# One transpose task for both token tiles of a normed projection, and tasks due close together issued together

## Chip, cores and metric

The kernel runs on one core of a Trainium2 chip. The metric is the device time of one execution in microseconds; a lower time is better. The time of before is the median of three runs. The profile is of one further execution.

## What is computed

Two layers of a decoder trunk over 256 tokens of width 1024. Each layer is a half-weighted SwiGLU feed-forward (hidden width 2816), a mixing stage with two groups of eight heads of 64 (group A in the code's order of work is the second half of the heads), and a second feed-forward. All of it is in float32. The mixing stages, cut to what matters here:

```python
def mix_stick_moba(xn, w_in, g_q_b, g_k_b, cos, sin):          # layer 0
    q, k, v = ...                                              # xn @ w_in, split in three, by heads
    out_a = stick_breaking_attention(q[:, :H_A], k[:, :H_A], v[:, :H_A])
    q_b = apply_rope(rms_norm(q[:, H_A:], g_q_b), cos, sin)
    k_b = apply_rope(rms_norm(k[:, H_A:], g_k_b), cos, sin)
    out_b = moba_attention(q_b, k_b, v[:, H_A:])
    ...

def mix_forget_dilated(xn, w_in, b_f, g_q_c, ..., cos, sin):   # layer 1
    log_f = log_sigmoid(proj[..., 3 * D_MIX:] + b_f)
    q_c = rms_norm(q[:, :H_C], g_q_c)                          # k_c likewise
    out_c = forgetting_attention(q_c, k_c, v[:, :H_C], log_f)
    q_d = apply_rope(rms_norm(q[:, H_C:], g_q_d), cos, sin)    # k_d likewise
    out_d = dilated_window_attention(q_d, k_d, v[:, H_C:])
    ...
```

A *normed projection* is a q or k that goes through `rms_norm` by head, with or without rope after it. There are six: q and k of the rope heads in both layers, and q and k of the forgetting heads in layer 1. They are called q2, k2 (rope) and q1, k1 (without).

## The kernel before, in words

The 256 tokens are two tiles of 128 (t = 0, 1). Weights stream in on the SP queue in units of 1 MB. Each unit is split into a high and a low part: ScalarE casts the high part (line 248), and VectorE subtracts it to get the low part (line 249). A projection is then three matmuls for each piece of weights, in `mm3` (line 149 is the one place that issues matmuls).

`token_major` projects 512 columns: first all of tile 0 (24 matmuls), then all of tile 1, and calls `done(t, ps)` after each. `project_norm` (line 481) uses it for a normed projection. Its `norm(t, ps)` squares on ScalarE (line 488), reduces on VectorE, takes a power on GpSimd (line 228), scales on VectorE into `qn` (line 493), and with rope forms `qs` on VectorE (lines 500 and 501) with products by GpSimd in between (line 498). The tags `qn`, `qs` and `sq` have two buffers each. Then TensorE transposes the tile, in 8 transposes (line 165, function `transposes`), into `tt`, a pair of PSUM banks of which there is one buffer, and ScalarE casts it into half of `qT` or `kT` (line 506).

The order on TensorE is written by hand; the other engines' order is left to the framework's scheduler. A small planner, `Weave`, keeps a clock `pe.t` that grows with each matmul by an assumed cost (its columns divided by 2400) and by 0.065 for a pair of transposes. Side work is a generator that is spawned as a task with a due time; where it yields x, it is due again x us later. `poll` is called after every three projection matmuls, and runs each task whose due time has passed, the earliest first. `join` runs tasks until given ones are done. `norm` is such a task: it yields 14 us (`LEAD_R`, with rope) or 10 us (`LEAD_N`) between its norm and its transposes, so that the norm is done by then.

A `Group` is the attention of eight heads and also a task, in six steps 6 us apart: scores `a` of a head pair (into two z banks, of which there are two buffers), transposes of the softmax `b` of the pair before, product `c` of the pair before that. The first group, A, waits until all norm tasks of q2 and k2 are done, looking every 0.2 us; the second, B, waits for q1, k1 and until A has issued four steps. In layer 1, `forget` also spawns a task: a chain over `lgy` on VectorE and ScalarE (lines 539 to 544), two small transposes (line 548), a cumulative sum of three small matmuls, and small copies.

In layer 0 the order in mixing is q2, k2, v2, q1, k1, v1, and the output projection of A, then that of B. In layer 1, `forget` stands between v2 and q1.

Of the kernel before, what the change touches and what calls it, by code (L numbers as in the profile page):

```python
# [11 lines left out]
AF = mybir.ActivationFunctionType  # L12
# [4 lines left out]
P = 128  # L17
TAIL = 3
LEAD_R, LEAD_N, LEAD_F, OVER = 14.0, 10.0, 8.0, 4
LEAD_X = (1.5, 1.5)  # L20
LEAD_0 = 3.0
PACE = ((6.0, 6.0), (6.0, 6.0))
HP = P // 2
D = 1024
KT = D // P
DFF = 2816
# [51 lines left out]
class Weave:  # L78
# [17 lines left out]
            self.tasks.remove(task)  # L96

    def poll(self):
        while self.tasks:
            task = min(self.tasks, key=lambda k: k[0])  # L100
            if task[0] > self.t:
                return
            self._run(task)

    def join(self, *tasks):
        while not all(k[2] for k in tasks):
            task = min(self.tasks, key=lambda k: k[0])
            self.t = max(self.t, task[0])
            self._run(task)
# [3 lines left out]
def trunk(ctx, tc, a, out):  # L113
    nc = tc.nc
# [12 lines left out]
    def nm(s):  # L127
        seen[s] = seen.get(s, 0) + 1
        return f"{s}_{seen[s]}"
# [13 lines left out]
    def pair():  # L143

        return psum.tile([P, 2, 512], F32, tag="tt", bufs=1, name=nm("tt"))
# [11 lines left out]
    def transposes(*srcs):  # L157

        tb, n, vs = pair(), 0, []
        for src in srcs:  # L160
            n0 = n
            for j in range(src.shape[-1] // P):
                for b in range(2):
                    r = slice(b * HP, (b + 1) * HP)
                    nc.tensor.transpose(tb[:, b, n * HP:(n + 1) * HP], src[r, j * P:(j + 1) * P], ident[r, r])  # L165
                n += 1
                pe.t += 0.065
            vs.append(tb[:, :, n0 * HP:n * HP].rearrange("p b (c t) -> p c b t", t=HP))
        return vs

    def halves(v):

        return v.rearrange("p c (b t) -> p c b t", t=HP)


    x = [keep.tile([P, D], F32, name=f"x{t}") for t in range(2)]
    ident = const.tile([P, P], F32, name="ident")
# [93 lines left out]
    class Normed:  # L271
# [16 lines left out]
        def transpose(self, t):  # L288
            tk, halfs = slice(t * P, (t + 1) * P), [slice(h * 512, (h + 1) * 512) for h in range(2)]
            for h, v in enumerate(transposes(*[x[t][:, sl] for sl in halfs])):  # L290
                kk = slice(4 * h, 4 * h + 4)
                xg = xpool.tile([P, 4, P], F32, tag="xg", bufs=2, name=nm("xg"))
                nc.vector.tensor_mul(halves(xg), v, self.g[:, kk].unsqueeze(2).unsqueeze(3).to_broadcast([P, 4, 2, HP]))  # L293
                nc.scalar.copy(self.hi[:, kk, tk], xg)  # L294
# [4 lines left out]
        def inverse(self, t):  # L299
            junk = xpool.tile([P, D], BF, tag="junk", name=nm("junk"))  # L300
            ss = small.tile([P, 1], F32, tag="ss", name=nm("ss"))
            nc.scalar.activation(junk, x[t], AF.Square, accum_out=ss)
            self.r[t] = rpow(ss, D, 1)
            if self.rb is None:
# [40 lines left out]
    def row_gemm(lhs, src, row0, tail, n_units, done, tasks=()):  # L345
# [16 lines left out]
        for u in range(n_units):  # L362
            r0 = row0 + 2 * u * P
            units.append(unit(src[r0:r0 + 2 * P, :].rearrange("(k p) n -> p k n", p=P), [2, D]))
            if u == 2:
# [90 lines left out]
    def _mix(mp, layer, xt, gains, done):  # L456
        def new(tag, width=512, bufs=2, dt=F32):
            return mp.tile([P, width], dt, tag=tag, bufs=bufs, name=nm(tag))
# [22 lines left out]
        def project_norm(c0, g, tag):  # L481
            qT = mp.tile([P, 4, SEQ], F32, tag=tag, bufs=2, name=nm(tag))
            tasks = []
            rope = isinstance(g, tuple)

            def norm(t, ps):
                sq = new("sq")
                nc.scalar.activation(sq, ps, AF.Square, scale=xt.r[t])
                ss = small.tile([P, 8], F32, tag="hss", name=nm("hss"))
                nc.vector.tensor_reduce(ss, heads(sq), axis=AX.X, op=ALU.add)  # L490
                r = rpow(ss, HD, 8)
                qn = new("qn")
                nc.vector.scalar_tensor_tensor(heads(qn), heads(ps), xt.r[t],  # L493
                                               r.unsqueeze(2).to_broadcast([P, 8, HD]), op0=ALU.mult, op1=ALU.mult)
                if rope:
                    gc, gs = g
                    o, sw = new("qs"), new("sq")
                    half_swap(lambda u, v: nc.gpsimd.tensor_mul(  # L498
                        heads(sw)[:, :, u], heads(qn)[:, :, v], over_heads(gs[:, t, u])))
                    nc.vector.tensor_mul(heads(o), heads(qn), over_heads(gc[:, t]))  # L500
                    nc.vector.tensor_add(o, o, sw)
                    yield LEAD_R
                else:
                    o = qn
                    yield LEAD_N
                nc.scalar.activation(halves(qT[:, :, t * P:(t + 1) * P]), transposes(o)[0], AF.Copy,
                                     scale=1.0 if rope else g)

            token_major(xt, w, c0, acc, lambda t, ps: tasks.append(pe.spawn(norm(t, ps))))
            return qT, tasks  # L510
# [210 lines left out]
        q2, tq = project_norm(cb, gq, "qT")  # L721
        k2, tk = project_norm(D + cb, gk, "kT")
        tc.keep_in_program_order(nc.scalar.preload_act_table_set("natural_log_exp_and_others"))
# [78 lines left out]
```

## Time and profile before

| | |
|---|---|
| median of three runs | 1029.31 us (1028.9 to 1030.21) |
| the profiled execution | 1029.01 us |
| span of the profile, first to last instruction | 1027.2 us |
| mean granted TensorE clock | 0.993 |
| TensorE busy | 1003.0 us, 5410 matmuls and transposes |
| VectorE busy | 603.3 us |
| ScalarE busy | 497.7 us |
| GpSimd busy | 87.9 us |

The span covers the two layers: mixing lies at about 198 to 324 us in layer 0 and at 698 to 836 us in layer 1, the rest is feed-forward. PE is TensorE, PEld its weight loads, DVE VectorE, ACT ScalarE, POOL GpSimd. A granted clock of 1.00 is TensorE at 2.4 GHz, 0.50 is 1.2 GHz. In the rows further down, a timeline row has the start in us, the time from the first to the last instruction in it, the engine, the line, and what was written from what; "[0.24 <-ACT pT L681]" is idle time ahead of it and what ended that. Matmuls overlap, so the step from one start to the next is what one costs in a row of them.

### The profile page before, as it was taken

Reading aid. Unit: us, or ns where it says so; the run is one execution under the profiler, and the core shown is the slowest. Engines: PE = TensorE matmul, PEld = TensorE weight load, DVE = VectorE, ACT = ScalarE, POOL = GpSimd, SP = SyncE. Lnnn points to the kernel's source line nnn. Section 1 sums busy time; section 2 is a strip of 40 time slices with the busy share of each in tenths; the row PEclk is TensorE's granted clock in tenths of the full one; section 3 lists DMA queues with packets and bytes.
Section 4 is the critical chain, followed back from the end, with each engine's and each line's share of the span. In section 5 each row is a group of like instructions: output and inputs, shape, how many; then the busy total and the mean of one; then the engine's idle time right before and its main releaser. Section 6 shows DMA issues by size and latency. Waiting matters only on the chain.

```text
span 1027.2 us, 13525 instructions
## 1 busy us (share of the span) xinstructions
PE 1003.0 (98%) x5410; PEld 833.3 (81%) x5410; DVE 603.3 (59%) x798; ACT 497.7 (48%) x669; POOL 87.9 (9%) x110
## 2 busy tenths in 40 slices
PE   7999999999999999999999999999999799999998
PEld 5888988779777888988878899887766678889886
DVE  6655554687676554564565546448876855546641
ACT  6554543555665444454454445336645555444530
POOL 0000200051000000000040000006431000000000
PEclk9999999999999999999999999999989999999999
DMA  9744475454233653655464456545523425535631
GB/s 331 266 154 153 159 284 187 158 187 165 83 127 123 211 185 123 215 212 198 142 230 164 150 178 245 185 145 196 175 84 103 144 82 194 205 124 205 216 123 41
DMA packets 81935, 175.95 MB, mean 171 GB/s; under 512 B 4544, under 2 KB 21264, under 8 KB 81872
## 3 DMA queue, kind: packets, MB, share of 16 engines
q1 hardware_dynamic: 80208, 174.86, 50.2%
q8 instruction: 42, 0.69, 0.3%
q0 software_dynamic: 512, 0.17, 0.2%
q10 hardware_dynamic: 1152, 0.06, 0.1%
q14 instruction: 21, 0.17, 0.0%
HBM read 173.99 MB, written 1.05 MB: 170 GB/s over the span
## 4 chain that ended last, share of the span: by engine, by line
PE 88%; DVE 6%; ACT 2%; issue 1%; POOL 1%; DMA 1%; SPq 0%; ACTq 0%; DVEq 0%; POOLq 0%
PE acc L149 54%; PE z L149 25%; PE o L149 6%; DVE lo L249 3%; PE tt L165 3%; ACT hi L248 1%; PE tt L149 1%; POOL rp L228 1%; POOL sq L498 1%; DMA raw<-in_w_in_ab 1%; DVE mx L663 0%; ACT t L669 0%; DMA x<-in_x 0%; DVE qn L493 0%; DVE xg L293 0%
## 5 line engine op out<-in xcount | busy, mean ns | idle before, releaser
L249 DVE TENSOR_TENSOR lo<-raw,hi 128x1024 fp32r<-128x1024 f32 (+2 forms) x348 | 403.4, 1171 | 240.5 <-ACT hi L248 229.8
L248 ACT CAST hi<-raw 128x1024 fp32r<-128x1024 f32 (+2 forms) x348 | 344.6, 1001 | 293.8 <-PE z L149 124.8
L149 PE MATMUL acc<-hi,xt 128*128 128x512 f32 (+1 forms) x1088 | 344.6, 387 | 3.9 <-ACT xt L294 2.1
L149 PEld LDWEIGHTS acc<-hi,xt 128*128 128x128 f32 x1088 | 204.4, 190 | 43.4 <-DVE xt L295 4.4
L149 PE MATMUL z<-hi,xt 128*128 128x512 f32 (+1 forms) x768 | 226.5, 371 | 0.0
L149 PE MATMUL acc<-lo,xt 128*128 128x512 f32 (+1 forms) x544 | 207.1, 381 | 0.0
L149 PEld LDWEIGHTS z<-hi,xt 128*128 128x128 f32 x768 | 142.4, 188 | 20.0
L149 PE MATMUL z<-lo,xt 128*128 128x512 f32 (+1 forms) x384 | 142.3, 371 | 0.0
L149 PEld LDWEIGHTS acc<-lo,xt 128*128 128x128 f32 x544 | 103.5, 190 | 15.6 <-DVE lo L249 0.2
L149 PE MATMUL acc<-hi,hh 128*128 128x512 f32 x264 | 103.6, 392 | 0.0
L149 PE MATMUL acc<-hi,hl 128*128 128x512 f32 x264 | 102.9, 390 | 0.0
L149 PE MATMUL acc<-lo,hh 128*128 128x512 f32 x264 | 102.8, 389 | 0.0
L228 POOL TENSOR_TENSOR rp<-ms,mhalf 128x1 f32<-128x1 f32 (+1 forms) x24 | 31.9, 1328 | 618.8 <-DVE ms L226 618.7
L149 PEld LDWEIGHTS z<-lo,xt 128*128 128x128 f32 x384 | 72.1, 188 | 9.9
L394 DVE TENSOR_TENSOR h<-z,sg 128x512 f32<-128x512 f32 (+1 forms) x48 | 30.9, 643 | 54.5 <-PE z L149 54.5
L149 PEld LDWEIGHTS acc<-hi,hh 128*128 128x128 f32 x264 | 49.5, 188 | 10.4
L149 PEld LDWEIGHTS acc<-hi,hl 128*128 128x128 f32 x264 | 49.5, 188 | 10.4
L149 PEld LDWEIGHTS acc<-lo,hh 128*128 128x128 f32 x264 | 49.5, 188 | 10.0
L390 ACT ACTIVATE sg<-acc,rp 128x512 f32<-128x512 f32 (+1 forms) x48 | 31.4, 654 | 41.3 <-PE acc L149 40.6
L263 ACT CAST hh<-tt 128x512 fp32r<-128x512 f32 (+1 forms) x48 | 26.5, 551 | 46.4 <-PE tt L165 26.7
L264 DVE TENSOR_TENSOR hl<-tt,hh 128x512 fp32r<-128x512 f32 (+1 forms) x48 | 31.0, 646 | 21.7 <-ACT hh L263 21.4
L149 PE MATMUL o<-hi,hh 128*128 128x512 f32 x88 | 34.4, 391 | 0.0
(144 smaller groups left out, 799.1 us busy)
## 6 DMA issues: line engine op xcount, KB each, us to landing
raw<-in_ffn_w_down SPq DMA_DIRECT2D x44, 1024.0 KB, 5.0
raw<-in_ffn_w_up SPq DMA_DIRECT2D x32, 1024.0 KB, 5.1
raw<-in_ffn_w_gate SPq DMA_DIRECT2D x30, 1024.0 KB, 5.1
raw<-in_ffn_w_gate SPq DMA_DIRECT2D x16, 768.0 KB, 4.4
raw<-in_ffn_w_up SPq DMA_DIRECT2D x16, 768.0 KB, 4.4
raw<-in_w_in_ab SPq DMA_DIRECT2D x12, 1024.0 KB, 5.3
raw<-in_w_in_cd SPq DMA_DIRECT2D x12, 1024.0 KB, 5.2
raw<-in_w_out SPq DMA_DIRECT2D x8, 1024.0 KB, 5.0
```

The source lines that it names most:

```text
L149: nc.tensor.matmul(o, lhsT, rhs, start=start, stop=stop, skip_group_check=True)
L165: nc.tensor.transpose(tb[:, b, n * HP:(n + 1) * HP], src[r, j * P:(j + 1) * P], ident[r, r])
L228: nc.gpsimd.tensor_tensor(r, m, mhalf[:, :width], op=ALU.pow)
L248: nc.scalar.copy(hi[:, j:j + m], w[:, i * n + j:i * n + j + m])
L249: nc.vector.tensor_sub(lo[:, j:j + m], w[:, i * n + j:i * n + j + m], hi[:, j:j + m].bitcast(F32))
L263: nc.scalar.copy(halves(hi), v)
L264: nc.vector.tensor_sub(halves(lo), v, halves(hi).bitcast(F32))
L390: nc.scalar.activation(sg[t][:, :n], pg[:, :n], AF.Silu, scale=xt.r[t])
L394: nc.vector.tensor_mul(hs[t][:, :n], pu[:, :n], sg[t][:, :n])
L498: half_swap(lambda u, v: nc.gpsimd.tensor_mul(heads(sw)[:, :, u], heads(qn)[:, :, v], over_heads(gs[:, t, u])))
```

## The change

`norm` of tile 0 now ends after the norm, and that of tile 1 transposes both tiles, in one set of 16, and casts both halves. `poll` also runs, after each task that it runs, all other tasks that are due within the next 0.5 us.

```diff
+SOON = 0.5
...
     def poll(self):
         while self.tasks:
             task = min(self.tasks, key=lambda k: k[0])
             if task[0] > self.t:
                 return
             self._run(task)
+            for k in sorted(self.tasks, key=lambda k: k[0]):
+                if k is not task and k[0] <= self.t + SOON and k in self.tasks:
+                    self._run(k)
...
+            outs = []
+
             def norm(t, ps):
...
                     nc.vector.tensor_add(o, o, sw)
-                    yield LEAD_R
                 else:
                     o = qn
-                    yield LEAD_N
-                nc.scalar.activation(halves(qT[:, :, t * P:(t + 1) * P]), transposes(o)[0], AF.Copy,
-                                     scale=1.0 if rope else g)
+                outs.append(o)
+                if t == 0:
+                    return
+                yield LEAD_R if rope else LEAD_N
+                for i, v in enumerate(transposes(*outs)):
+                    nc.scalar.activation(halves(qT[:, :, i * P:(i + 1) * P]), v, AF.Copy, scale=1.0 if rope else g)
```

## Rows read from the trace of the kernel before

**Rows 1.** The page's busy times, share of the span, instructions.
```profile
PE 1003.0 (98%) x5410; PEld 833.3 (81%) x5410; DVE 603.3 (59%) x798; ACT 497.7 (48%) x669; POOL 87.9 (9%) x110
```

**Rows 2.** Windows: stretch, its length, each engine's busy time, granted clock, DMA share, GB/s.
```profile
192.00:262.00 70.00, 69.30 (x463) 59.01 (x462) 55.89 (x88) 40.01 (x68) 20.40 (x15) 1.00 0.49 166
...
691.00:775.00 84.00, 79.92 (x459) 62.32 (x459) 69.02 (x142) 48.22 (x72) 36.34 (x33) 0.96 0.43 139
...
740.00:742.00 2.00, 0.65 (x7) 0.44 (x6) 1.21 (x2) 1.42 (x4) 0.00 (x0) 1.00 1.01 357
...
762.00:766.00 4.00, 4.00 (x10) 3.13 (x11) 1.20 (x4) 0.69 (x1) 0.00 (x0) 0.50 0.02 4
775.00:785.00 10.00, 8.41 (x47) 5.52 (x45) 6.14 (x12) 4.19 (x6) 2.07 (x1) 0.83 0.60 211
```

**Rows 3.** Waits of PE from 690 to 840: total, times, longest.
```profile
PE z L149 <- ACT kT L506: 2.1, 2, 1.4
```

**Rows 4.** Timeline of PE, layer 0, around a set of 16 and one of 8.
```profile
199.08 0.39 PE L149 MATMUL acc<-lo,xt 128*128 128x512 f32 x1
...
200.00 0.39 PE L149 MATMUL acc<-hi,xt 128*128 128x512 f32 x1
200.31 0.71 PE L165 MATMUL tt<-ident,x 64*128 64x64 f32 x16
...
201.29 0.40 PE L149 MATMUL acc<-lo,xt 128*128 128x512 f32 x1
...
221.17 0.39 PE L149 MATMUL acc<-hi,xt 128*128 128x512 f32 x1
221.49 0.47 PE L165 MATMUL tt<-ident,qs 64*128 64x64 f32 x8
...
222.22 0.39 PE L149 MATMUL acc<-lo,xt 128*128 128x512 f32 x1
```

**Rows 5.** Timeline of ACT and PE, layer 0, the last kT cast and A's first scores.
```profile
240.07 0.60 ACT L506 ACTIVATE kT<-tt 128x512 f32<-128x512 f32 x1 [3.43 <-PE tt L165]
...
241.10 0.92 PE L149 MATMUL z<-kT,qT 64*128 64x256 f32 x8
```

**Rows 6.** Timeline of DVE, ACT and PE, layer 1, ahead of A's first scores.
```profile
738.88 0.41 DVE L539 TENSOR_TENSOR lgy<-acc,rb 8x256 f32<-8x256 f32 x1
...
739.70 0.42 ACT L541 ACTIVATE lge<-lgy 8x256 f32<-8x256 f32 x1 [2.20 <-DVE lgy L540]
...
740.91 0.57 ACT L506 ACTIVATE kT<-tt 128x512 f32<-128x512 f32 x1
...
741.54 0.92 PE L149 MATMUL z<-kT,qT 64*128 64x256 f32 x8 [1.35 <-ACT kT L506]
```

**Rows 7.** Timeline of PE and DVE, layer 0: q2's second set, k2's first `qs`.
```profile
227.55 0.46 PE L165 MATMUL tt<-ident,qs 64*128 64x64 f32 x8
...
228.29 1.23 DVE L500 TENSOR_TENSOR qs<-qn,gc 128x512 f32<-128x512 f32 x1
```

**Rows 8.** Timeline of PE, layer 1: transposes that wait.
```profile
758.21 0.51 PE L165 MATMUL tt<-ident,t 64*128 64x64 f32 x6 [1.27 <-DVE t L673]
...
761.30 0.69 PE L165 MATMUL tt<-ident,qn 64*128 64x64 f32 x8 [0.24 <-ACT pT L681]
761.92 0.79 PE L149 MATMUL acc<-hi,xt 128*128 128x512 f32 x1
...
772.34 0.46 PE L165 MATMUL tt<-ident,qn 64*128 64x64 f32 x8 [0.76 <-ACT pT L681]
...
778.34 0.60 PE L165 MATMUL tt<-ident,t 64*128 64x64 f32 x6 [1.59 <-DVE t L673]
```

**Rows 9.** Timeline of PE and DVE, layer 0: B's first scores, A's last transposes.
```profile
268.99 0.27 PE L149 MATMUL z<-negb,identb 128*128 128x256 bf16 x1 [1.26 <-ACT t L669]
...
270.20 1.01 DVE L673 TENSOR_SCALAR t<-t,l 128x128 f32<-128x128 f32 x4
...
272.09 0.59 PE L165 MATMUL tt<-ident,t 64*128 64x64 f32 x12
```

## The prediction, made before the changed kernel ran

> **What bounds the kernel now.** I read the page's busy times first: TensorE is busy for 98% of the span, so a change of its instruction order is worth what it takes from, or adds to, TensorE's own sequence [rows 1]. Next the windows by stage: the change acts in the two mixing stages alone. In layer 0's, TensorE is busy 69.3 of 70 us; in layer 1's first part only 79.9 of 84 us, and there VectorE is busy 69.0 us [rows 2]. So layer 0 is bound by TensorE, and layer 1 partly by what VectorE and ScalarE hand to it. The waits and timelines say where: for the kT casts (line 506) 2.1 us in two waits [rows 3], of which 1.35 us stand ahead of group A's first scores [rows 6]; for the softmax ahead of A's transposes 1.27 and 1.59 us, and for the `tt` banks 0.24 and 0.76 us ahead of two transposes of qn [rows 8].
>
> **The order that the change makes.** I worked it out from the planner's due times (0.213 us of its clock for a 512-column matmul, a poll after every three). All four feed-forward parts keep their order. In mixing, each of six projections has its two sets of 8 transposes replaced by one set of 16, where about the second stood. The 0.5 us rule moves three things: in layer 0, A's last transposes and third product join group B's first scores, with 0.7 us less of matmuls between A's last scores and them than before; in layer 1, the lgy transposes follow A's first transposes instead of preceding A's second scores, so the cumulative sum stands alone; and A's later steps no longer drag the first set of q1 behind them. The sum is made against the profiled execution, 1029.01 us (span 1027.2), which is 0.3 us under the median of the runs, 1029.31.
>
> *One set of transposes among projection matmuls.* Matmuls follow each other at (200.00 - 199.08)/4 = 0.23 us. A set of 8 stretches the two steps around it to 222.22 - 221.17 = 1.05 us, 0.59 more than 0.46. A set of 16 takes 201.29 - 200.00 = 1.29, 0.83 more [rows 4]. Joining two sets saves 2 x 0.59 - 0.83 = 0.35 us of TensorE. Layer 0 has two joined sets: **-0.7** (ends: -0.7, and 0 if TensorE then waits anyway).
>
> *The second cast, layer 0.* Both halves of kT are now cast after the 16 transposes. Before, A's scores began at 241.10 and the one cast, 0.60 us, started at 240.07, with 0.43 us to spare [rows 5]. One more cast of 0.60 overshoots by 0.17: **+0.2** (ends 0 and +0.6). The casts of qT are read 10 us later and cost nothing; if that cover were gone, 0.6 us each.
>
> *B's first scores with A's last transposes, layer 0.* TensorE waits 1.26 us for the z bank at 268.99, and the transposes at 272.09 follow softmax divisions that end at 270.20 + 1.01 [rows 9]. Issued together, the break into the matmuls goes once less (about half of the 0.59 above, 0.3), but the transposes come up before the divisions are done, so that most of the wait moves there: **-0.4** (ends: -1.7, wait and break both gone, and +0.6, the transposes wait out the divisions).
>
> *Layer 1's rope projections.* TensorE would again save 0.7 us, but A's first scores start when the kT cast ends; that cast stands behind ScalarE's share of lgy, which begins at 739.70, and this behind VectorE's lgy at 738.88 [rows 6]. An earlier TensorE only waits longer: 0. With two casts behind them, +0.57, the duration in that row: **+0.6** (ends: -2.05, 0.7 and the whole 1.35, if both casts run ahead of lgy's share; +1.15 if one more instruction as long as the cast stands between).
>
> *A's steps, layer 1.* Between A's second scores and their transposes there are three matmuls fewer, and these transposes wait already (1.27) [rows 8]: 3 x 0.23 = +0.7. For its last transposes the cover grows by the 8 more of the joined set, 0.25: -0.25. The cumulative sum's own break, from nothing to 0.59: +0.2, as it has 3 small matmuls and no bank to wait for. Together **+0.6** (ends 0 and +1.0).
>
> *q1.* Its first set, from 761.30 to the next matmul at 761.92 [rows 8], goes out of A's step: -0.6. The second, with its 0.76 us wait, costs 0.59 + 0.76 = 1.35 and becomes a set of 16 without that wait, 0.83; but these 0.5 us stand ahead of A's last transposes, which wait for VectorE anyway (1.59). **-0.6** (ends -1.1 and 0).
>
> *k1 and group B.* -0.35 for the join; B's first scores already wait the rest of the 2.1 us, 0.75 [rows 3], for one cast, and a second adds about 0.7, as these casts carry a gain (up from 0.6 in [rows 5], and no more than twice that): **+0.35** (ends -0.35 and +0.85).
>
> *Buffers.* `qs` has two buffers, held until the joined transposes. k2's first write of `qs` came at 228.29, after q2's second set at 227.55 [rows 7], where the joined set will be: 0 (a VectorE wait of 0.3 at most, covered by splits done ahead; without this cover 0.3). The planner adds no DMA and moves none on a queue; the evacuations keep their number.
>
> The sum is -0.7 + 0.2 - 0.4 + 0.6 + 0.6 - 0.6 + 0.35 = 0.05 us, nothing that shows: I take 1029.1 us. The ends add to -5.9 and +4.2.
>
> The Trainium skill, page "Perfetto Trace Analysis", section "Optimizing Scalar/DVE Operations", says that where these engines aren't saturated but cause bubbles elsewhere, breaking instructions up may let work complete sooner; joining is the opposite. The trace bears it out in kind: ScalarE is busy 48%, and its kT casts hold TensorE up. By that rule alone the sum would be the three second casts, +1.5 us; by the rows it is offset.
>
> **Rivals.** *Faster.* The joins count in full and ScalarE takes the two casts ahead of the lgy chain: -0.7 - 0.4 - 2.05 - 1.1 - 0.35 + 0.6 + 0.2 = -3.8. If in addition the last wait of A shrinks, and the clock stays up there, more: that stretch has a granted clock of 0.83, and at the half level (1.2 GHz, [rows 2]) 10 matmuls took 4.0 us, 0.4 each instead of 0.23. Ten at half clock are 1.7 us. Time: 1025.3, or 1023.6. For it: TensorE's 98%. Against it: the scheduler put the cast behind the lgy chain once already.
>
> *Slower.* A's first scores in layer 1 wait for two casts, and the granted clock falls to the half level behind that wait, as it did behind the waits of 1.27 and 0.24 us up to 761.30 and around the 1.59 us wait [rows 2, 8]. The wait there is now 1.35, and the clock is at its full level, 2.4 GHz (1.00 from 740 to 742) [rows 2, 6]. With 1.95 us in its place it could fall: 10 to 16 matmuls at 0.17 more, 1.7 to 2.7 us. Time: 1029.1 + 2.7 = 1031.8. It decides from the point where that wait is about as long as the 1.59 us one; which of these it resembles no row settles.
>
> *It does less than it says.* If tasks due together are ordered as before, only the joins remain: -0.7 + 0.2 + 0.6 - 0.6 + 0.35 = -0.15, 1028.9. It isn't told apart from my forecast by time.
>
> **How the numbers follow.** About 0.2% (2.1 us) is what a measurement of this kernel can tell from no change. The forecast and the rival that does less have 0.44, with a range of their own of 1027.2 to 1031.4. The faster rival has 0.30: five of the seven terms have ends below zero, and TensorE is the bound. The slower one has 0.26, nearly all of it the clock and the casts. Range: 1025.3 to 1032.3, from the faster rival's time to the slower one's with half a microsecond of a longer wait; the ends of all terms at once lie outside.
>
> **What would show it.** Right: six sets of 16 transposes at line 165 from qs and qn, none of 8; in layer 0 less than 0.3 us of waiting for kT and the transposes of A right behind B's first scores, with a wait for `t`; in layer 1 a kT wait of about 1.9 us ahead of A's first scores and 1.4 ahead of B's; no wait for pT ahead of qn's transposes. Wrong: kT casts ahead of the lgy chain, or a stretch at half clock in layer 0 or at 740, or VectorE waiting several us to write qs.

## The result, and the profile after

The changed kernel takes 1019.82 us (median of four runs, 1019.26 to 1020.84) against 1029.23 for the kernel before in the same comparison: a ratio of 0.9907, 95% interval 0.9895 to 0.9919. I had forecast 1029.1, with a range down to 1025.3. The profiled execution took 1019.7 us, its span is 1017.9. Medians are of the fast executions; one of e14, of 1995.47 us, is left out of its median. The page of the profile shows a TensorE with as many instructions, 6.6 us less of busy time and 2.7 us less of idle time; the other engines have the work they had [rows 1]:

```profile
PE 996.4 (98%) x5410; PEld 830.4 (82%) x5410; DVE 602.4 (59%) x798; ACT 496.4 (49%) x669; POOL 88.6 (9%) x110
```

To find where 9.4 us went I read the starts of six landmarks from TensorE's timeline, in both traces and later in all others: the first transposes of x at either end of a mixing stage, and the scores of groups A and B. Layer 0's stage went from 116.44 to 115.41 us, 1.03 less, where 0.9 less was forecast. The feed-forwards kept their time. Layer 1's stage went from 132.32 to 123.16, 9.16 less, where 0.95 more was forecast. These are its landmarks after, with A's second scores (747.07) and two waits that come up below:

```profile
699.27 0.71 PE L171 MATMUL tt<-ident,x 64*128 64x64 f32 x16
...
740.16 0.92 PE L155 MATMUL z<-kT,qT 64*128 64x256 f32 x8 [1.55 <-ACT kT L517]
...
747.07 0.92 PE L155 MATMUL z<-kT,qT 64*128 64x256 f32 x8
...
750.75 0.60 PE L155 MATMUL acc<-cst,lg 128*8 128x128 f32 x4 [0.58 <-DVE lg L560]
...
754.78 0.92 PE L155 MATMUL z<-kT,qT 64*128 64x256 f32 x8
...
756.55 0.60 PE L171 MATMUL tt<-ident,t 64*128 64x64 f32 x6 [0.45 <-DVE t L683]
...
763.25 0.92 PE L155 MATMUL z<-kT,qT 64*128 64x256 f32 x8
...
786.93 0.92 PE L155 MATMUL z<-kT,qT 64*128 64x256 f32 x8 [0.23 <-ACT kT L517]
...
822.43 0.71 PE L171 MATMUL tt<-ident,x 64*128 64x64 f32 x16
```

In the kernel before the landmarks stand at 699.43, 741.54, 756.01, 768.60, 797.04 and 831.75. The stretches between them, in us, for all kernels of this study (e14 is the kernel of e15). The startup differs by up to 1.6 us from profile to profile, and the stretches don't have that in them. "The first stretch" is below the one from A's third to its fourth scores, "the second" the one from there to B's first:

| kernel | x to A's 1st scores | to A's 3rd | to A's 4th | to B's 1st | to x of the feed-forward |
|---|---|---|---|---|---|
| before | 42.11 | 14.47 | 12.59 | 28.44 | 34.71 |
| changed | 40.89 | 14.62 | 8.47 | 23.68 | 35.50 |
| e1 joins alone | 40.96 | 14.49 | 9.62 | 24.54 | 35.85 |
| e2 rule alone | 41.84 | 14.62 | 8.34 | 25.79 | 35.61 |
| e3 before, lgy later | 42.19 | 15.44 | 8.48 | 28.44 | 34.65 |
| e4 changed, lgy earlier | 40.89 | 13.79 | 13.44 | 23.67 | 35.35 |
| e5 before, one fill | 42.11 | 14.45 | 10.33 | 28.46 | 34.68 |
| e6 before, two fills | 42.10 | 14.47 | 10.35 | 26.88 | 34.88 |
| e7 before, splits moved | 42.13 | 14.48 | 12.57 | 25.70 | 34.50 |
| e8 before, more of them moved | 42.10 | 14.51 | 8.25 | 25.69 | 34.85 |
| e9 changed, product first | 39.29 | 14.80 | 8.42 | 23.66 | 36.76 |
| e10 changed, fill that waits | 40.88 | 14.60 | 8.42 | 23.66 | 38.64 |
| e11 changed, cast on VectorE | 41.18 | 14.58 | 8.44 | 24.06 | 35.39 |
| e12 before, mean first | 41.35 | 14.48 | 11.82 | 28.46 | 36.07 |
| e13 changed, fills in the tail | 40.90 | 14.58 | 8.41 | 23.68 | 34.79 |
| e15 e9 with fills in the tail | 39.28 | 14.83 | 8.45 | 23.66 | 34.78 |

The stretches don't all hold the same work. Counted in the timelines, the changed kernel has three projection matmuls (0.7 us, at 0.23 each [rows 4]) fewer ahead of A's first scores, three fewer from there to the third, three more to the fourth, as many to B's first, and three more behind these. With the matmuls counted out at that price, I estimate that its stretches changed by -0.5, +0.8, -4.8, -4.8 and +0.1 us. e4, e9 to e11, e13 and e15 are laid out like the changed kernel; e3, e5 to e8 and e12 like the kernel before. Against before, e1 has three more to A's fourth scores and three fewer to B's first; e2 has three fewer to A's first and three fewer to its third, and six more to B's first.

Two stretches carry 8.9 of the 9.2 us: those behind A's third and fourth scores. Ahead of the transposes there, the waits of before are 1.27, 0.25, 0.24, 0.76 and 1.59 us (all but the 0.25 in [rows 8]); after, one of 0.45 is left, and the clock stays up. The windows of [rows 2], after:

```profile
691.00:775.00 84.00, 81.22 (x498) 63.49 (x496) 73.03 (x151) 51.02 (x76) 36.18 (x33) 1.00 0.45 152
740.00:742.00 2.00, 1.84 (x12) 1.53 (x13) 0.65 (x3) 0.67 (x3) 0.00 (x0) 1.00 1.00 376
762.00:766.00 4.00, 4.00 (x40) 2.96 (x39) 2.71 (x10) 1.54 (x4) 1.10 (x1) 1.00 0.00 0
775.00:785.00 10.00, 10.00 (x50) 7.95 (x48) 5.07 (x7) 4.33 (x6) 2.62 (x1) 1.00 0.28 103
```

762 to 766 had a clock of 0.50 and 10 matmuls; now it has 1.00 and 40, among them short ones (scores and transposes). 775 to 785 had 0.83 and 8.41 us of work; now 1.00 and no idle time. VectorE is busier in the same 84 us, as more of its work falls into them.

Why the softmax of A's second scores is ready earlier shows in VectorE's timeline. The first fence has these scores before, on TensorE; after, they are at 747.07. The second fence is VectorE before, the third VectorE after:

```profile
748.71 0.92 PE L149 MATMUL z<-kT,qT 64*128 64x256 f32 x8
```

```profile
747.89 1.23 DVE L249 TENSOR_TENSOR lo<-raw,hi 128x1024 fp32r<-128x1024 f32 x1 [0.44 <-ACT hi L248]
...
749.25 1.23 DVE L249 TENSOR_TENSOR lo<-raw,hi 128x1024 fp32r<-128x1024 f32 x1
...
753.66 1.20 DVE L249 TENSOR_TENSOR lo<-raw,hi 128x1024 fp32r<-128x1024 f32 x1
...
756.54 1.19 DVE L249 TENSOR_TENSOR lo<-raw,hi 128x1024 fp32r<-128x1024 f32 x1
...
757.79 0.53 DVE L673 TENSOR_SCALAR t<-t,l 128x128 f32<-128x128 f32 x2
```

```profile
747.23 1.23 DVE L255 TENSOR_TENSOR lo<-raw,hi 128x1024 fp32r<-128x1024 f32 x1 [0.76 <-ACT hi L254]
...
751.06 1.22 DVE L255 TENSOR_TENSOR lo<-raw,hi 128x1024 fp32r<-128x1024 f32 x1
...
753.62 1.19 DVE L255 TENSOR_TENSOR lo<-raw,hi 128x1024 fp32r<-128x1024 f32 x1
...
755.18 0.53 DVE L683 TENSOR_SCALAR t<-t,l 128x128 f32<-128x128 f32 x2
```

The long rows are weight splits of 1.2 us, for projections that come later; the last row is the first division for A's second head pair, for which its transposes wait. Before, four splits are near: the first starts 0.8 us ahead of the scores, three follow them; after, it is three, the first right behind the start of the scores. The first division starts 9.08 us behind the scores before and 8.11 after. At the same time the cover grew, that is, the time that TensorE has other work for: its third scores, after which the transposes come, start 7.71 us behind the second for 7.30, though three matmuls fewer stand between, since the cumulative sum now has a break and a wait of 0.58 us of its own there. The two, 0.97 and 0.41, make up for the wait of 1.27. Ahead of the last divisions of A's fourth pair there are three splits before (773.52, 775.51, 776.86) and one after (769.21). No line of the diff touches a split. The scheduler orders VectorE's and ScalarE's queues anew when TensorE's order changes, and here its new order puts the softmax further forward.

### The profile page after: what moved, and what is told of

The parts are those of the page before. It is cut to its first block, busy times and chain, and to the rows that moved or that the text cites. A ratio compares the mean times of both kernels' runs of the same rounds, so it can differ in the third digit from the quotient of the medians.

```text
span 1017.9 us, 13520 instructions
## 1 busy us (share of the span) xinstructions
PE 996.4 (98%) x5410; PEld 830.4 (82%) x5410; DVE 602.4 (59%) x798; ACT 496.4 (49%) x669; POOL 88.6 (9%) x110
## 3 DMA queue, kind: packets, MB, share of 16 engines
HBM read 173.99 MB, written 1.05 MB: 172 GB/s over the span
## 4 chain that ended last, share of the span: by engine, by line
PE 89%; DVE 5%; ACT 2%; issue 1%; POOL 1%; DMA 1%; SPq 0%; ACTq 0%; DVEq 0%; POOLq 0%
PE acc L155 54%; PE z L155 25%; PE o L155 6%; PE tt L171 3%; DVE lo L255 3%; ACT hi L254 1%; PE tt L155 1%; POOL rp L234 1%; POOL sq L506 1%; DMA raw<-in_ffn_w_gate 1%; DMA raw<-in_w_in_ab 1%; DVE qn L501 0%; ACT t L679 0%; DVE mx L673 0%; DVE t L683 0%
## 5 line engine op out<-in xcount | busy, mean ns | idle before, releaser
L155 PE MATMUL acc<-hi,xt 128*128 128x512 f32 (+1 forms) x1088 | 340.8, 384 | 4.6 <-ACT xt L300 3.3
```

The costliest lines, as they stand in the source:

```text
L155: nc.tensor.matmul(o, lhsT, rhs, start=start, stop=stop, skip_group_check=True)
```

## Experiments

**The parts alone.** e1 has the joined sets without the rule for tasks due together; e2 has the rule and not the joined sets.

```diff
             task = min(self.tasks, key=lambda k: k[0])
...
             self._run(task)
-            for k in sorted(self.tasks, key=lambda k: k[0]):
-                if k is not task and k[0] <= self.t + SOON and k in self.tasks:
-                    self._run(k)
```

> The joined transposes without the 0.5 us rule. Theory S (the rule moves A's steps in layer 1 three matmuls forward, so that VectorE has one weight split less ahead of the softmax divisions, the waits shrink and the clock stays up): this kernel keeps the old place of A's second step, so its transposes still wait about 1.3 us and the stretch at half clock behind them stays; of the 9.4 us it has at most 4: 1025 to 1028 us. Theory M (the joined sets do it: no transposes of qn inside A's steps, no waits for the tt banks): nearly all of the gain, 1019.5 to 1022 us, and no stretch at half clock from 750 to 790.

> The 0.5 us rule without joined transposes. Theory S: most of the gain, 1020 to 1024 us; the wait ahead of A's second transposes in layer 1 is under 0.6 us and no half clock follows it. Theory M: nothing much, 1027 to 1030 us, with the waits of 0.2 and 0.8 us ahead of the transposes of qn still there.

e1 measured 1020.81 us (ratio 0.9919, 0.9905 to 0.9934), e2 1023.6 (0.9947, 0.993 to 0.9964). Either part alone takes most of the gain, 8.4 and 5.6 us of 9.4, so they are two ways to the same place and their gains don't add. In both, the two stretches at half clock are gone; their last stretch is about 1 us longer than before's, at a mean clock of 0.91 (e1, 789 to 825) and 0.86 (e2, 790 to 826) for 0.95 (before, 797 to 832). They don't do it in the same manner: in e1 A's second transposes wait as long as before, and the clock doesn't fall.

```profile
756.91 0.51 PE L168 MATMUL tt<-ident,t 64*128 64x64 f32 x6 [1.27 <-DVE t L680]
757.68 0.60 PE L168 MATMUL tt<-ident,t 64*128 64x64 f32 x6 [0.26 <-DVE t L680]
...
768.17 0.71 PE L168 MATMUL tt<-ident,qn 64*128 64x64 f32 x16 [0.84 <-ACT pT L688]
```

```profile
760.00:765.00 5.00, 5.00 (x30) 3.89 (x31) 2.76 (x11) 1.59 (x2) 0.44 (x1) 1.00 0.00 0
```

The first fence is e1's TensorE, the second its window behind these waits. From x to A's first scores, e1 is 1.15 us shorter with before's number of matmuls, so this comes with the joins. e2 is 0.27 shorter, which is less than the three matmuls (0.7) that it has fewer there: the rule alone gains nothing in this stretch.

**Where the lgy transposes stand.** The rule moves them behind A's first transposes. A due time does that too: `LEAD_F` 8.0 to 8.6 in the kernel before (e3), and 8.0 to 7.7 in the changed one to put them back ahead (e4).

```diff
-LEAD_R, LEAD_N, LEAD_F, OVER = 14.0, 10.0, 8.0, 4
+LEAD_R, LEAD_N, LEAD_F, OVER = 14.0, 10.0, 8.6, 4
```

> The kernel before with the lgy task's delay 8.6 in place of 8.0: the lgy transposes follow A's first transposes and the cumulative sum stands alone, as in the changed kernel, and nothing else moves. Theory L (it is the place of the lgy work that frees VectorE ahead of A's second transposes): the wait there falls from 1.5 us to about 0.5, the first half-clock stretch goes, 1024 to 1027 us. Theories S and M: no change, 1028.5 to 1030 us.

> The changed kernel with the lgy task's delay 7.7: the lgy transposes ahead of A's second scores and the sum in the same break, as before the change. Theory L: the wait ahead of A's second transposes is back at 1.3 us or more with the half clock behind it, 1022 to 1025 us. Theories S and M: no loss, or 0.5 us gained as the sum's own wait of 0.58 us goes, 1019 to 1020.5 us.

e3 measured 1025.92 (0.9969, 0.9957 to 0.9981): the first stretch goes from 12.59 to 8.48, and 0.97 of that is lost in the one ahead of it; the second, with its 1.59 us wait, stays at 28.44. e4 measured 1023.9 (0.9948, 0.9933 to 0.9963): the first stretch is back at 13.44, behind waits of 2.29 and 0.24 us, with a clock of 0.51 from 760 to 765, and 0.83 is gained ahead of it; the second stays at 23.67. So the place of the lgy transposes sets the wait in the first stretch, and does not touch the second, which either part of the change shortens alone (e1, e2). Theory L's times came, but not for its reason: in e3 VectorE is no freer, with four splits and the first division 9.42 us behind the second scores (before 9.08). It is the cover that grew, from 7.30 to 8.53 us between the second and third scores, and the wait is 0.29. In e4 the cover is 6.62.

**The wait or the clock behind it.** e5 is the kernel before with 28 small matmuls, whose result nobody reads, in TensorE's wait ahead of A's second transposes; VectorE's, ScalarE's, GpSimd's and SP's orders are those of before. e6 has the same ahead of A's fourth transposes too.

```diff
             def soft_b(self, p):
+                if self.kind == "dil" and p in (1,):
+                    fill = pair()
+                    for i in range(28):
+                        nc.tensor.matmul(fill[:, i % 2, 0:P], identb, negb[:, 0], start=True, stop=True,
+                                         skip_group_check=True)
```

> The kernel before, with 28 extra small matmuls (128 columns, bfloat16, into the tt banks, overwritten by what follows) ahead of A's second transposes in layer 1. They fill the wait of 1.27 us there and shorten no wait; VectorE's and ScalarE's order is as before. Theory C (most of the gain is TensorE's clock, which falls behind that wait): the granted clock stays at 1.00 from 759 to 766, and 2.5 to 4 us go: 1025 to 1027 us. Theory W (the waits themselves are what was gained): no gain, 1029 to 1030.5 us.

> The same fill ahead of A's second and of A's fourth transposes in layer 1. Theory C: both stretches at half clock go, 1022 to 1025 us, though no wait is shorter. Theory W: 1029 to 1031 us.

e5 measured 1026.64 (0.9972, 0.9963 to 0.9982), e6 1025.91 (0.9967, 0.9955 to 0.9979), 0.9 above the range expected for e6: adding work made the kernel faster. By time alone e6 can't be told from e5, so what the second fill gains is read from the stretches. The clock in the windows of before, e5 and e6, a fence each:

```profile
760.00:765.00 5.00, 4.76 (x23) 3.45 (x20) 3.20 (x13) 1.86 (x4) 0.00 (x0) 0.50 0.01 3
...
780.00:785.00 5.00, 5.00 (x20) 3.29 (x18) 2.08 (x3) 2.30 (x4) 2.07 (x1) 0.67 0.52 194
```

```profile
760.00:765.00 5.00, 4.01 (x42) 2.91 (x40) 5.00 (x23) 2.73 (x6) 1.68 (x1) 1.00 0.23 86
...
780.00:785.00 5.00, 5.00 (x25) 3.25 (x26) 2.46 (x4) 2.21 (x3) 2.39 (x1) 0.72 0.44 168
```

```profile
760.00:765.00 5.00, 4.07 (x31) 3.11 (x32) 3.92 (x18) 2.10 (x4) 0.57 (x1) 1.00 0.04 9
...
780.00:785.00 5.00, 5.00 (x33) 3.42 (x32) 3.33 (x5) 2.06 (x3) 2.62 (x1) 1.00 0.22 82
```

Each fill mends its own stretch. The first gains 12.59 - 10.33 = 2.26 us, though TensorE then waits 0.69 longer for the `tt` bank (0.93 for 0.24), so that I estimate the clock's own cost at about 2.9; the second gains 28.46 - 26.88 = 1.58.

**The queue order.** e7 and e8 are the kernel before with TensorE's order untouched. The weight splits of A's output projection are queued behind A's fourth softmax: in e7 those of its second unit (`free=1`; three splits go from ahead of the last divisions), in e8 those of all units (`free=0`), which also takes the last of the four, at 756.54, and its cast from ahead of A's second divisions.

```diff
+            with ExitStack() as queue:
+                if behind["free"] <= 0:
+                    for ins in behind["ins"]:
+                        queue.enter_context(tc.issue_after(ins))
+                behind["free"] -= 1
+                for j in range(0, n, m):
+                    nc.scalar.copy(hi[:, j:j + m], w[:, i * n + j:i * n + j + m])
+                    nc.vector.tensor_sub(lo[:, j:j + m], w[:, i * n + j:i * n + j + m], hi[:, j:j + m].bitcast(F32))
...
+        if layer == 1:
+            behind.update(ins=(late["exp", 3].ins, late["div", 3].ins), free=1)
         out_rows(first.lhs, a["w_out"][layer], cb)
```

> The kernel before, with three weight splits of A's output projection (casts on ScalarE, subtractions on VectorE) queued behind the softmax of A's last step in layer 1, where two or three stood ahead of its last divisions; TensorE's order is as before. Theory O (the wait of 1.59 us ahead of A's last transposes is made by the order in VectorE's and ScalarE's queues): the wait falls below 0.2 us, the half clock around 780 goes, 1024 to 1026.5 us. Rival (the wait is made by the sets of q1 in TensorE's order): no gain, 1028.5 to 1030 us.

> As the run before, and the one split that directly precedes the divisions of A's second step queued behind too, so that three splits and not four stand between that step's scores and its divisions, as in the changed kernel. Theory O: the waits of 1.27 and 0.25 us ahead of A's second transposes fall to about 0.4, and the first stretch at half clock goes as well: 1020.5 to 1023.5 us, without a joined set or the 0.5 us rule. Rival: 1028.5 to 1030 us.

e7 measured 1027.66 (0.9982, 0.9972 to 0.9991), 1.2 above its expected range though the wait of 1.59 us and the half clock around 780 are gone; e8 measured 1023.44 (0.9942, 0.9928 to 0.9957). In e8 the waits for `t` are gone and both stretches are at full clock; these are all of its waits between A's third and B's first scores that TensorE's timeline shows:

```profile
760.17 0.47 PE L165 MATMUL tt<-ident,qn 64*128 64x64 f32 x8 [0.36 <-ACT pT L687]
768.95 0.46 PE L165 MATMUL tt<-ident,qn 64*128 64x64 f32 x8 [0.75 <-ACT pT L687]
777.39 0.86 PE L149 MATMUL o<-pT,v 128*64 128x256 f32 x6 [0.20 <-ACT pT L687]
```

One split moved takes 4.34 us from the first stretch (12.59 to 8.25, the changed kernel has 8.47). Against e5, which has only the clock right, 2.08 of that are the waits themselves. The three take 2.74 from the second (28.44 to 25.70); against e6, 1.18 are the wait. What is left to the changed kernel's 23.68 is 2.0: the wait of 0.75 that is no longer there, 0.55 less in the wait for B's kT (0.23 for 0.78), 0.6 less around A's last transposes and last product, which in e8 takes 1.65 us with the wait of 0.20 inside and 0.80 in the changed kernel, and 0.1 for the sets themselves (three of 8 at 0.59 against two of 16 at 0.83 [rows 4], as the first of q1's sets of 8 stood in the first stretch). How much of the 2.0 comes with the joins was not isolated.

**The 1.2 us ahead of A's first scores.** With the joined sets, the chain up to lgy and kT ends earlier. In the changed kernel VectorE reduces k2's second tile ahead of the rope product of the first; e9 puts the product first again. (The expectation says group B's keys: the edit is in k2, whose scores group A makes.)

```diff
-                nc.vector.tensor_reduce(ss, heads(sq), axis=AX.X, op=ALU.add)
+                with tc.issue_after(mul.pop().ins) if mul else ExitStack():
+                    nc.vector.tensor_reduce(ss, heads(sq), axis=AX.X, op=ALU.add)
...
-                    nc.vector.tensor_mul(heads(o), heads(qn), over_heads(gc[:, t]))
+                    product = nc.vector.tensor_mul(heads(o), heads(qn), over_heads(gc[:, t]))
+                    if t == 0 and layer == 1 and tag == "kT":
+                        mul.append(product)
```

> The changed kernel with one order put back: in layer 1 the reduction of the second token tile of group B's first keys waits in VectorE's queue behind the rope product of the first token tile, as the kernel before has it; TensorE's order is untouched. Theory Q (the 1.2 us by which A's first scores of layer 1 come earlier come from VectorE meeting GpSimd's powers later in its queue, so that it waits 1.7 and 1.1 us less there): the stretch from the first transposes of x1 to A's first scores goes from 40.89 us back to 41.8 to 42.2, and the time is 1020.5 to 1021.2. Rival (the 1.2 us come from the transposes that TensorE no longer issues): the stretch stays within 0.2 of 40.89 and the time between 1019 and 1020.3.

e9 measured 1019.02 (0.9901, 0.9888 to 0.9914). Theory Q falls, and the stretch is outside the rival's band too: 39.29, another 1.6 less. The scheduler moved more than the edit names, and what it moved shows on ScalarE, in e9:

```profile
737.32 1.09 ACT L520 ACTIVATE kT<-tt 128x512 f32<-128x512 f32 x2 [1.06 <-PE tt L171]
738.76 0.41 ACT L554 ACTIVATE lge<-lgy 8x256 f32<-8x256 f32 x1 [0.35 <-DVE lgy L553]
```

In this order the two casts run ahead of lgy's share, and TensorE doesn't wait for kT at all. In the changed kernel they stand behind it:

```profile
737.84 0.42 ACT L551 ACTIVATE lge<-lgy 8x256 f32<-8x256 f32 x1 [1.48 <-DVE lgy L550]
738.29 0.42 ACT L552 ACTIVATE lge<-lge 8x256 f32<-8x256 f32 x1
738.74 0.41 ACT L553 ACTIVATE lge<-lge 8x256 f32<-8x256 f32 x1
739.06 1.05 ACT L517 ACTIVATE kT<-tt 128x512 f32<-128x512 f32 x2
```

e12 takes the next difference: a split between k2's first sum and its mean (VectorE of before, then of the changed kernel).

```profile
721.16 1.22 DVE L249 TENSOR_TENSOR lo<-raw,hi 128x1024 fp32r<-128x1024 f32 x1
722.30 0.17 DVE L226 TENSOR_SCALAR ms<-hss 128x8 f32<-128x8 f32 x1
```

```profile
721.01 0.17 DVE L232 TENSOR_SCALAR ms<-hss 128x8 f32<-128x8 f32 x1
721.08 2.36 DVE L255 TENSOR_TENSOR lo<-raw,hi 128x1024 fp32r<-128x1024 f32 x2
```

```diff
-                nc.vector.tensor_sub(lo[:, j:j + m], w[:, i * n + j:i * n + j + m], hi[:, j:j + m].bitcast(F32))
+                with tc.issue_after(behind["ins"][0]) if behind["ins"] and behind["free"] < 0 else ExitStack():
+                    nc.vector.tensor_sub(lo[:, j:j + m], w[:, i * n + j:i * n + j + m], hi[:, j:j + m].bitcast(F32))
...
+            behind.update(ins=[late["k2"]], free=1)
             q1, tq = project_norm(ca, gains[1][0], "qT")
+            behind.update(ins=[])
```

> The kernel before with one weight split moved in VectorE's queue in layer 1: the second half of q1's first weights is queued behind the mean square of k2's first token tile (kernel before: ahead of it, 721.16 to 722.30), and with it one split moves behind k2's last rope product; the order on TensorE, ScalarE, GpSimd and SP stays as it was. Theory R (that split, 1.14 us, delays the mean, GpSimd's power and with them the whole chain up to lgy and kT; in the changed kernel it stands behind the mean): the stretch from the first transposes of x1 to A's first scores falls from 42.11 to 40.9 to 41.2 us, and the time by 0.5 to 1.2 us, to 1028.0 to 1028.8. Rival (the gain there comes from the transposes that TensorE no longer issues, or from ScalarE's cast that goes): the stretch stays between 41.9 and 42.2, and the time within 0.4 of the kernel before.

e12 measured 1028.69 (0.9993, 0.9984 to 1.0002). The stretch is 41.35, between the bands and nearer to theory R: this swap and the other split that moves with it, with TensorE's order untouched, are worth 0.76 of the 1.22 us. TensorE waits for kT at the end of the stretch in before, e12 and the changed kernel, so it is this chain that sets the stretch. The other 0.46 was not isolated. The time hardly moved: the profile fell on the slowest of eleven runs (1030.51), and its last stretch is 36.07 for 34.71, with a clock of 0.59, 0.50 and 0.63 in the windows from 816 to 828.

**The casts.** e11 puts the second cast of each normed key on VectorE.

```diff
-                    nc.scalar.activation(halves(qT[:, :, i * P:(i + 1) * P]), v, AF.Copy, scale=1.0 if rope else g)
+                    if i == 1 and tag == "kT":
+                        nc.vector.tensor_scalar(halves(qT[:, :, i * P:(i + 1) * P]), v, 1.0 if rope else g, None,
+                                                op0=ALU.mult)
+                    else:
+                        nc.scalar.activation(halves(qT[:, :, i * P:(i + 1) * P]), v, AF.Copy, scale=1.0 if rope else g)
```

> The changed kernel with the second cast of each normed key's transposes on VectorE in place of ScalarE. Theory S (the two casts of layer 1's first keys, 0.5 us each and one behind the other on ScalarE, stand last before A's first scores): the wait there falls from 1.55 to about 1.0 us, and the time is 1019 to 1019.5. Rival (VectorE has the same place occupied by weight splits and rope steps, so that the cast comes no earlier, or the steps behind it come later): 1019.8 to 1021.

1020.81 (0.9921, 0.9909 to 0.9933): the rival. The scheduler put the cast behind the last step of lgy on VectorE, and the wait grew from 1.55 to 1.79, and for B's kT from 0.23 to 0.61.

**The tail.** In the changed kernel the clock still falls once, behind waits of 2.31 and 1.62 us in group B. e10 puts fills there, into the `tt` bank; e13 into one of the three `acc` banks, which are long free; e14 and e15 are e9 with e13's edit.

```diff
+            def fill(self, n):
+                b = acc()
+                for i in range(n):
+                    nc.tensor.matmul(b[:, 0:P], identb, negb[:, 0], start=True, stop=True, skip_group_check=True)
...
             def soft_a(self, p):
+                if self.lf and p == 3:
+                    self.fill(34)
...
             def soft_b(self, p):
+                if self.lf and p == 3:
+                    self.fill(22)
```

> The changed kernel with 40 small matmuls, whose result nobody reads, ahead of group B's fourth scores and 28 ahead of its fourth transposes in layer 1, where TensorE waits 2.31 and 1.62 us and the granted clock behind them is 0.60. Clock theory (a wait there costs once more through the clock behind it): the stretch 812 to 816 us shows a clock of 1.00, and the time falls by 0.8 to 1.5 us, to 1018.3 to 1019.2. Rival (the clock costs nothing there, since TensorE waits for ScalarE and VectorE anyway, or the added matmuls take what the clock gives): 1019.8 to 1020.5.

> The changed kernel with 34 small matmuls, whose result nobody reads, ahead of group B's fourth scores and 22 ahead of its fourth transposes in layer 1. They write a bank that is long free, so that they stand inside TensorE's waits of 2.31 and 1.62 us (0.06 us each, 2.1 and 1.3 us). Clock theory (a wait there costs once more through the granted clock behind it): 812 to 816 us has a clock of 1.00 in place of 0.60, the stretch from B's first scores to x0's transposes falls from 35.50 to 34.0 to 34.8 us, and the time to 1018.3 to 1019.3. Rival (what TensorE loses there to the lower clock it would lose waiting anyway): the stretch stays at 35.3 or more and the time between 1019.5 and 1020.3.

> The kernel with the rope product ahead of the reduction (whose first scores come 1.6 us earlier than the changed kernel's, and whose tail takes 36.76 us in place of 35.50, at a clock of 0.50 to 0.69 from 804 to 816) with the same small matmuls in the tail. Clock theory (the earlier gain was given back to the clock in the tail): the clock from 804 to 816 is 1.00, the tail takes 34.0 to 34.8 us, and the time is 1016.6 to 1017.6, under both the kernel before and the changed one. Rival (the tail's 1.3 us more have another cause, such as a weight split in VectorE's queue): the tail stays over 36 us and the time over 1018.5.

> The same kernel as before this one, taken again, since the profile of its first run fell on an execution of 1995 us in which every matmul took about twice its time, and shows nothing of the question. Clock theory: the clock from 800 to 824 is 1.00, the stretch from B's first scores to x0's transposes is 34.0 to 34.9 us (36.76 without the small matmuls), and the time 1016.6 to 1017.8. Rival: that stretch stays over 36 us and the time over 1018.5.

e10 measured 1022.44 (0.9931, 0.9919 to 0.9943), slower than without its fills, and tells nothing of the clock: its fills waited themselves, and ran at a clock of 0.61 (805 to 809) ahead of the scores.

```profile
805.41 4.00 PE L653 MATMUL tt<-negb,identb 128*128 128x128 bf16 x40 [1.84 <-ACT pT L701]
```

e13 measured 1018.68 (0.9891, 0.9875 to 0.9908); the last stretch is 34.79 for 35.50, and the window 812 to 816 has a clock of 1.00 for 0.60. e14 and e15 are one kernel: 1017.42 and 1017.5 (0.9883, 0.9866 to 0.9899, and 0.9885, 0.9868 to 0.9901). It is the fastest of this study, though its interval meets the changed kernel's. Windows of e9, then of e15:

```profile
804.00:808.00 4.00, 3.62 (x34) 2.63 (x33) 2.73 (x11) 1.85 (x10) 0.00 (x0) 0.69 0.23 88
808.00:812.00 4.00, 3.32 (x26) 2.15 (x24) 2.79 (x9) 1.92 (x7) 0.00 (x0) 0.50 0.00 0
812.00:816.00 4.00, 4.00 (x15) 2.76 (x12) 0.69 (x1) 0.58 (x1) 0.00 (x0) 0.53 0.00 0
```

```profile
804.00:808.00 4.00, 3.51 (x49) 2.59 (x47) 2.73 (x12) 2.09 (x9) 0.00 (x0) 1.00 0.34 130
808.00:812.00 4.00, 3.09 (x39) 1.98 (x38) 2.80 (x10) 2.01 (x7) 0.00 (x0) 1.00 0.03 6
812.00:816.00 4.00, 4.00 (x21) 3.13 (x21) 0.91 (x2) 0.59 (x1) 0.00 (x0) 1.00 0.00 0
```

The last stretch goes from 36.76 to 34.78. So most of what e9's earlier scores gained (1.6) had been given back here (1.26). The clock went up with the fills, but the scheduler also moved a few rows of VectorE and ScalarE in this stretch, among them the divisions in e13 and the cast of `oh` in e15, so the 0.71 and 1.98 us aren't the clock's alone for certain.

## Why the prediction was wrong

The forecast was 0.05 us more, and 9.4 less were measured. Layer 0 came out. In layer 1 the prediction took the order in VectorE's and ScalarE's queues as fixed, and gave the half clock behind two waits no term.

*Layer 0: right.* 1.03 us less, forecast 0.9. The joins gave 0.58 (e1; forecast 0.7 less 0.2 for the second cast), the rule another 0.45 on top of them (forecast 0.4), though by itself it gives 0.05 (e2). A's scores don't wait for the two kT casts, and the 1.26 us wait for a z bank [rows 9] moved to the transposes, as the prediction said:

```profile
240.54 0.92 PE L155 MATMUL z<-kT,qT 64*128 64x256 f32 x8
...
270.53 0.60 PE L171 MATMUL tt<-ident,t 64*128 64x64 f32 x6 [1.21 <-DVE t L683]
```

*"Layer 1's rope projections", +0.6: wrong sign.* The stretch is 1.22 shorter, or 0.5 with the three matmuls counted out that now follow these scores, which the prediction's list of what the rule moves doesn't have. "An earlier TensorE only waits longer: 0" took VectorE's row of lgy as a fixed time. It is a place in a queue, and the queue was ordered anew: lgy starts 37.76 us behind the first transposes of x, for 39.45. e12 shows 0.76 of this from two splits. The second cast cost what was said, 1.05 us for two; the wait only grew from 1.35 to 1.55, since lgy comes earlier and TensorE too. The kT waits are 1.8 us in two [rows 3], where some 3.3 were forecast:

```profile
PE z L155 <- ACT kT L517: 1.8, 2, 1.5
```

*"A's steps, layer 1", +0.6: the step that failed most.* Three matmuls less of cover did not lengthen the wait for `t` by 0.7: it went from 1.27 to nothing for the first half of these transposes and 0.45 for the second. The prediction held VectorE's queue fixed, but the first division comes 0.97 earlier behind the scores; and it gave the cumulative sum "no bank to wait for", but the sum waits 0.58 us for `lg`, which with its own break made the cover 0.41 longer and not 0.7 shorter. The sum's price stands in the stretch from A's first to its third scores: about 0.8 (0.15 longer with three matmuls less), where 0.2 was forecast. And no term held the clock behind that wait: the prediction had the half-clock window among its rows and used it in rivals alone. Of the 4.34 us that the first stretch loses in e8, 2.26 go when the clock alone is mended (e5), and 2.08 with the waits.

*"q1", -0.6, and "k1 and group B", +0.35.* The second stretch lost 4.8 us. As forecast, q1's first set went out of A's step and the 0.76 us wait is gone. But the prediction counted nothing for the 0.5 us behind that, as A's last transposes "wait for VectorE anyway (1.59)": this wait is gone, and the clock behind it stays up, which by e7 alone is worth 2.74 (1.58 of it the clock, by e6). And it added 0.7 for a second cast at B, where the wait fell from 0.78 to 0.23.

*"Buffers", 0.* VectorE never waited for `qs`, as forecast. Whether the longer hold of `qs` is what made the scheduler choose another order was not tried.

*The rivals.* The faster one had "the clock stays up" at 1023.6, and the condition it set, casts ahead of the lgy chain, did not come true in the changed kernel; e9, where it did, shows the 1.6 us that it would have given. The slower one had the clock fall behind A's first scores; with a wait of 1.55 us there, 740 to 742 shows 1.00. The result lies 3.8 us under the lowest time that any rival had.

The Trainium skill, page "Perfetto Trace Analysis", section "Optimizing Scalar/DVE Operations", speaks for breaking instructions up; by that rule alone the sum was +1.5; 9.4 us less were measured, for reasons other than the casts. The Trainium skill, page "PSUM — Partial Sum Buffer", section "Engine vs sequencer instructions", says that the queues of ScalarE, VectorE and GpSimd are strict first in, first out. That is the rule that was wanted here: by it a division is as late as the splits ahead of it, and the rows of VectorE above agree, with 1.2 us for each split.

*What stays open.* The same waits of 1.27 and 0.25 us are followed by half clock in the kernel before and not in e1. The wait of 0.24 and the set of 8 that follow in the former alone, up to 761.30, come too late to be the reason, against the prediction's reading of the rows: the clock is 0.71 from 759 to 760 and 0.50 from 760 to 761. Nor does it look like an accident of one profile, as the mean clock is 0.996 or 0.997 in all four runs of e1, and 0.992 to 0.995 in those of the kernel before, but for one. What decides was not found. Nor has any run the changed kernel's order on TensorE with before's order on VectorE: what the queue order is worth is shown in the kernel before (e7, e8), and taken from there for the changed one.

## What to carry to other kernels

Where the other engines' order is made by a scheduler, a change of TensorE's order is also a change of theirs: what an engine does ahead of a critical instruction is not a constant of the profile. Price a wait of a TensorE that is otherwise full twice, once as the wait and once as the clock behind it, and look for work in VectorE's queue that is early (here weight splits) and stands ahead of work that is late. Judge by stretches between landmarks, and count the matmuls in them: a gain early in a stage can be given back at its end, or be work that only moved.

## What the runs showed of the hardware

The clock's price was of the size of the waits' themselves: about 2.9 us behind waits of 1.27 and 0.25 (e5), 1.58 behind one of 1.59 (e6), and up to 1.98 behind 2.31, 0.19 and 0.52 (e15 against e9). Matmuls whose result nobody reads, put into the waits, bought it back. The Trainium skill, page "TensorE: Matmul & The Clock Gate", section "HAM oscillation — how this bites in real kernels", tells of a kernel that pays for a slowed clock again after each wait for a DMA; the trace agrees in kind, at 0.50 behind the wait of 1.27 us and 0.67 from 780 to 785, behind that of 1.59, though here the waits are for VectorE. Falls of the clock also differ from run to run of one kernel: of e12's eleven runs, the four with a mean granted clock of 0.995 took 1026.71 to 1027.54 us, the seven with 0.991 to 0.993 took 1028.34 to 1030.51.
